# A hybrid decoder layer on one core: memory's first quarter in two pieces, the first weight slice scaled on VectorE

## The chip, the core and the metric

The kernel runs on one core of a Trainium2 chip. The core has TensorE (PE, matrix products; its weight loads are shown as PEld), VectorE (DVE), ScalarE (ACT), GpSimd (POOL) and SyncE (SP), which here only issues transfers. Engines run side by side and wait for each other by semaphores; the queue of each engine is in order. SBUF is the working memory, PSUM the memory of eight banks into which TensorE writes. The metric is the device time of one execution in microseconds.

## The reference

One layer with three groups of heads side by side, a residual and a final norm:

```python
h = rmsnorm(x, ln_g)                        # x: 1024 x 2048
proj = h @ w_in                             # columns split among the groups
out_a = gmlp_spatial_gating(...) * silu(g_z)            # 4 groups x 128
out_b = rmsnorm(gated_delta_rule(...)) * silu(d_z)      # 8 heads x 128, a recurrence over chunks of 64
m = rmsnorm(mem, mem_norm_g)                # mem: 256 x 2048
mk, mv = split(m @ w_mem_kv)                # keys and values of the memory, 4 heads x 128 each
out_c = softmax(c_q @ mk.T / sqrt(128)) @ mv * silu(c_z)
y = rmsnorm(x + concat(out_a, out_b, out_c) @ w_out, final_g)
```

All data is float32. The change touches the product `m @ w_mem_kv`.

## The kernel before

Matrix products are made from pairs of rounded numbers: every operand `t` is split into a high part `hi` (rounded to the type float32r by a cast) and a low part `lo = t - hi`, and `triple` (line 465) issues three products, hi by hi, hi by lo and lo by hi, into the same PSUM bank. Splitting is done by `split_to` (line 442): a cast on ScalarE, then a subtraction on VectorE.

The program isn't issued as it is written. Every instruction goes into a list (`Plan.add`, line 138) with its estimated cost, its rank and what it depends on; `Plan.issue` (line 228) plays the list through, engine by engine, always taking the ready instruction of the lowest rank, and then issues all of them in that order (line 297, the line that the profile shows for nearly everything). The order on each engine is fixed from then on. Since it comes from one sweep over all estimated times, an edit at the start can change the order far behind it.

The work around the change is the start of the kernel, the memory stage:

- `load_mem(q)` (line 495) loads quarter `q` of the memory's 2048 columns: two tiles of 128 rows by 512 columns, called `kT` (rows 0 to 127) and `qT` (rows 128 to 255) in the profile, 256 KB each, both issued by SyncE. Lines 516 to 525 set the order: quarter 0, the gain `mem_norm_g` on ScalarE's queue (8 KB), weight slices 0 and 1, quarter 1, weight slices 2 and 3, quarters 2 and 3.
- Seven small products of a tile of ones (`warm`, line 540) keep TensorE occupied until the gain is there; the gain is transposed into `gcol`, one column for each slice of 128 input columns.
- `spread_mem(q)` (line 546) transposes a quarter on TensorE, four 128x128 blocks into one PSUM bank for each of the two row tiles. Two banks, `dn_111` and `dn_112`, take turns for this (`spare`, line 530). Each bank is split into the high part (a tile of the ring `gt`) and the low part (a tile of the ring `inv`).
- The loop at line 595 runs over the 16 weight slices `k`, 128 rows by 1024 columns each (512 KB). `load_kv` loads a slice into one of four buffers (two `wraw`, two `ut`), slice 0 as two halves; ScalarE scales it by the gain into `whi`, VectorE computes the low part `wlo` from the raw slice, the gain and `whi`; TensorE does 12 products of 256 columns for the keys (banks `acc`) and 6 of 512 columns for the values (banks `dn`). Two buffers hold `whi` and `wlo` in turn, so slice k + 2 waits for the products of slice k.
- In between stand the squares of the memory's rows for its norm (ScalarE, `jk`), and `prep` (line 557): x's row tiles (`vs`, `kd`, then `kT`, `qT` again) are loaded, squared, scaled, transposed through the same two banks and, for the first half of x's rows here, copied to `tn`, split and written out (`put0`). `spare`'s two banks thus are shared by memory, x and a few small products.

Behind the memory stage follow the wide projections (`acc<-ahi,whi` and its like), cut into blocks, with the delta rule's inverses (`dn<-inv`), its scan (`dn<-tblk,gt`, `dn<-states,kT`, `dn<-steps,...`) and the spatial gate (`dn<-wsT,el`) strewn between their products, then attention and the output projection.

Of the kernel before, what the change touches and what calls it, by code (L numbers as in the profile page):

```python
# [11 lines left out]
AF = mybir.ActivationFunctionType  # L12
ALU = mybir.AluOpType
# [4 lines left out]
P = 128  # L18
# [4 lines left out]
HT = 512  # L23
# [37 lines left out]
class Plan:  # L61
# [27 lines left out]
    @contextmanager  # L89
    def rank(self, cls):  # L90
        old, self.cls = self.cls, cls
        yield
        self.cls = old

    @contextmanager
    def behind(self, op):
        old, self.gate = self.gate, op
        yield
        self.gate = old
# [201 lines left out]
def kernel(  # L301
# [21 lines left out]
    x, mem, w_in, out = x[0], mem[0], w_in[0], out[0]  # L323
# [7 lines left out]
    V, S, G, PE, Q = R.dve, R.act, R.pool, R.pe, R.sp  # L331
    rank, behind = R.rank, R.behind

    def C(shape, name, dt=F32):
        return sb.tile(list(shape), dt, name=name, tag=name)[:]
# [44 lines left out]
    def tok(ap):  # L380

        return ap.rearrange("p (t c) -> p t c", c=P)
# [38 lines left out]
    def tpb():  # L421
        turn["tp"] += 1
        return acc[2 + turn["tp"] % 2]
# [5 lines left out]
    ident, ones, utri = (C([P, P], n) for n in ("ident", "ones", "utri"))  # L429
# [12 lines left out]
    def split_to(hi, lo, src, eng):  # L442
        S.copy(hi, src)
        eng.tensor_tensor(out=lo, in0=src, in1=hi, op=ALU.subtract)
# [20 lines left out]
    def triple(a, l, r, start, stop, cls=9):  # L465

        mm(a, l[0], r[0], start, False, cls)
        mm(a, l[0], r[1], False, False, cls)
        return mm(a, l[1], r[0], False, stop, cls)
# [4 lines left out]
    def row_scale(xq):  # L474

        s = small()
        for c in range(4):
            S.activation(jk, xq[c], AF.Square, accum_out=s[:, c : c + 1])
        V.tensor_reduce(s[:, 4:5], s[:, 0:4], axis=AX.X, op=ALU.add)
        V.tensor_scalar(s[:, 4:5], s[:, 4:5], 1.0 / D, EPS, op0=ALU.mult, op1=ALU.add)  # L480
        rsqrt_to(s[:, 5:6], s[:, 4:5])
        return s[:, 5:6]


    def row_tiles(tag):
        if tag in ("inv", "gt", "ut"):
            return [b[:, i * HT : (i + 1) * HT] for b in (ring[tag](), ring[tag]()) for i in range(2)]
        return [ring[tag]() for _ in range(4)]
# [3 lines left out]
    mem_rows = [row_tiles("kT"), row_tiles("qT")]  # L492
    x_rows = {}

    def load_mem(q):
        for mt in range(2):
            Q.dma_start(mem_rows[mt][q], mem[mt * P : (mt + 1) * P, q * HT : (q + 1) * HT])

    def kv_parts(k):
        n = XW if k == 0 else 2 * XW  # L500
        return [slice(i, i + n) for i in range(0, 2 * XW, n)]

    def load_kv(k):
        for sl in kv_parts(k):
            Q.dma_start(kvraw[k % 4][:, sl], w_mem_kv[k * P : (k + 1) * P, sl])

    def load_x(tt, tag, after=(None,) * 4):
        x_rows[tt] = row_tiles(tag)
        for c in range(4):
            with behind(after[c] or R.gate):  # L510
                Q.dma_start(x_rows[tt][c], x[tt * P : (tt + 1) * P, c * HT : (c + 1) * HT])
# [2 lines left out]
    rows = y1.rearrange("p c m -> p (c m)")[:, 0:P]  # L514
    mrow = rows[0:16]
    with rank(2):
        load_mem(0)
        S.dma_start(mrow, mem_norm_g[0].rearrange("(c p) -> c p", p=P))
        for k in range(4):
            load_kv(k)  # L520
            if k == 1:
                load_mem(1)
    with rank(3):
        load_mem(2)
        load_mem(3)
# [4 lines left out]
    def spare():  # L530
        turn["dn"] = 1 - turn["dn"]
        return flip[turn["dn"]]
# [10 lines left out]
    gcol = C([P, 16], "gcol")  # L543
    with rank(1):
        V.tensor_copy(gcol, pt[:, 0:16])
    def spread_mem(q):
        h, l = (ring[t](F32R).rearrange("p (k n) -> p k n", k=4) for t in ("gt", "inv"))
        for mt in range(2):
            tp = spare()
            for k in range(4):  # L550
                PE.transpose(tp[:, k * P : (k + 1) * P], mem_rows[mt][q][:, k * P : (k + 1) * P], ident)
            sl = slice(mt * P, (mt + 1) * P)
            with rank(2):
                split_to(h[:, :, sl], l[:, :, sl], tok(tp), V)
        return h, l

    def prep(tt, put, bank):

        xq = x_rows[tt]
        r = row_scale(xq)  # L560
        for q in range(NQ):
            V.scalar_tensor_tensor(xq[q], xq[q], r, gb[q], op0=ALU.mult, op1=ALU.mult)
            tp = bank()
            for k in range(4):
                PE.transpose(tp[:, k * P : (k + 1) * P], xq[q][:, k * P : (k + 1) * P], ident)
            put(q, tok(tp))
# [8 lines left out]
    def put0(tt):  # L575
        def put(q, tp):
            if tt >= H0:
                with rank(1):
                    split_to(ahq[q][:, tt], alq[q][:, tt], tp, V)
                return  # L580
            t = tok(ring["tn"]())
            with rank(1):
                S.copy(t, tp)
            with rank(2):
                split_to(ahq[q][:, tt], alq[q][:, tt], t, V)
            with rank(5):
                Q.dma_start(h0_d[4 * q : 4 * q + 4, :, tt * P : (tt + 1) * P].rearrange("k p n -> p k n"), t)

        return put


    rm = []
    kvmark = []
    mhl = [spread_mem(0)]
    for k in range(KT):
        mh, ml = mhl[k // 4]
        if k >= 4:
            with rank(3):
                load_kv(k)
        hi, lo = kvhi[k % 2], kvlo[k % 2]  # L600
        with rank(2):
            for sl in kv_parts(k):
                raw = kvraw[k % 4][:, sl]
                S.activation(hi[:, sl], raw, AF.Copy, scale=gcol[:, k : k + 1])
                V.scalar_tensor_tensor(lo[:, sl], raw, gcol[:, k : k + 1], hi[:, sl], op0=ALU.mult, op1=ALU.subtract)
        kk = k % 4
        for h in range(NX):
            sl = slice(h * P, (h + 1) * P)
            triple(ka[h][:, :NMEM], (hi[:, sl], lo[:, sl]), (mh[:, kk], ml[:, kk]), k == 0, k == KT - 1)
        for mt in range(2):  # L610
            sl = slice(mt * P, (mt + 1) * P)
            triple(va[mt], (mh[:, kk, sl], ml[:, kk, sl]), (hi[:, XW:], lo[:, XW:]), k == 0, k == KT - 1)
        kvmark.append(R.ops[-1])
        if k == 3:
            with rank(2), behind(kvmark[-1]):
                for c in range(4):
                    Q.dma_start(gb[c], ln_g[0, c * HT : (c + 1) * HT].partition_broadcast(P))
        if k in (1, 4, 8):
            with behind(kvmark[-1]):
                mhl.append(spread_mem(len(mhl)))  # L620
        if k == 1:
            load_x(0, "vs", kvmark[1:2] * 4)
        if k == 3:
            for mt in range(2):
                rm.append(C([P, 1], f"rm{mt}"))
                V.tensor_copy(rm[mt], row_scale(mem_rows[mt]))
        if k == 4:
            load_x(1, "kd", kvmark[4:5] * 4)
        if k == 5:
            prep(0, put0(0), spare)  # L630
        if k == 7:

            dg, rmb = (ring["E"]()[:, 0:NMEM] for _ in range(2))
            for mt in range(2):
                V.tensor_scalar(dg[:, mt * P : (mt + 1) * P], ident, rm[mt], None, op0=ALU.mult)
            pt = spare()
            PE.matmul(pt[:, 0:NMEM], ones, dg, start=True, stop=True)
            S.copy(rmb, pt[:, 0:NMEM])
        if k == 9:
            prep(1, put0(1), spare)  # L640
            load_x(2, "kT", (kvmark[6], kvmark[7], kvmark[7], kvmark[8]))
        if k == 13:
            load_x(3, "qT", (kvmark[10], kvmark[11], kvmark[11], kvmark[12]))
            with rank(2):
                prep(2, put0(2), spare)
# [584 lines left out]
    a = tpb()  # L1230
# [23 lines left out]
    a = tpb()  # L1254
# [564 lines left out]
```

## Time and profile before

| | us |
|---|---|
| three runs | 1626.97, 1629.00, 1629.74 |
| median | 1629.0 |
| profiled execution, its own time | 1630.94 |
| span of the profile (first to last instruction) | 1629.2 |
| TensorE busy | 1611.6 |
| VectorE busy | 1262.2 |
| ScalarE busy | 1027.0 |
| GpSimd busy | 300.3 |

A row of the order of time reads: start, duration, engine, line, operation, output <- inputs, shapes, count, and in brackets the idle time of the engine before it and what ended that. An engine's name with a q (SPq) is an instruction of its queue, the issue of a transfer; the transfer itself lands later. In the waits each row names who waited for whom, with the total, the number of times and the longest. A view by stretches gives for each engine the busy time within a stretch and the number of instructions, then the TensorE clock that was granted, the mean busy share of the DMA engines and the transferred GB/s. Matrix instructions overlap, so their durations add up to more than the time between their starts.

### The profile page before, as it was taken

Reading aid. Unit: us, or ns where it says so; the run is one execution under the profiler, and the core shown is the slowest. Engines: PE = TensorE matmul, PEld = TensorE weight load, DVE = VectorE, ACT = ScalarE, POOL = GpSimd, SP = SyncE. Lnnn points to the kernel's source line nnn. Section 1 sums busy time; section 2 is a strip of 40 time slices with the busy share of each in tenths; the row PEclk is TensorE's granted clock in tenths of the full one; section 3 lists DMA queues with packets and bytes.
Section 4 is the critical chain, followed back from the end, with each engine's and each line's share of the span. In section 5 each row is a group of like instructions: output and inputs, shape, how many; then the busy total and the mean of one; then the engine's idle time right before and its main releaser. Section 6 shows DMA issues by size and latency. Waiting matters only on the chain.

```text
span 1629.2 us, 26133 instructions
## 1 busy us (share of the span) xinstructions
PE 1611.6 (99%) x8576; PEld 1354.8 (83%) x8576; DVE 1262.2 (77%) x2100; ACT 1027.0 (63%) x2217; POOL 300.3 (18%) x482
## 2 busy tenths in 40 slices
PE   8999999999999999999999999999999999999997
PEld 8988888888888888888888788888888888888886
DVE  5966787879756567899988897768768888789775
ACT  6767675765475457888685346766666775344355
POOL 0101220351452010225235005330100000000001
PEclk9999999999999999999999999999999999999999
DMA  9867898988977785689878977878968869688646
GB/s 309 241 179 225 280 301 251 278 282 309 359 257 242 261 283 190 204 286 368 281 243 253 320 228 241 266 265 296 319 201 274 282 218 364 207 273 293 218 146 239
DMA packets 277227, 428.94 MB, mean 263 GB/s; under 512 B 31017, under 2 KB 102242, under 8 KB 277090
## 3 DMA queue, kind: packets, MB, share of 16 engines
q1 hardware_dynamic: 254338, 366.81, 68.7%
q0 software_dynamic: 22144, 59.40, 10.9%
q8 instruction: 67, 1.10, 0.3%
q10 hardware_dynamic: 608, 1.06, 0.2%
q14 instruction: 70, 0.57, 0.1%
HBM read 339.57 MB, written 87.06 MB: 262 GB/s over the span
## 4 chain that ended last, share of the span: by engine, by line
PE 89%; DMA 6%; DVE 2%; issue 1%; ACT 1%; SPq 1%; POOLq 0%; POOL 0%; DVEq 0%; ACTq 0%
PE acc L297 69%; PE dn L297 20%; DMA wraw<-in_w_in_dram 1%; SPq L297 1%; DMA vs<-od 1%; DMA kT<-in_mem_dram 1%; DVE alo L297 0%; DMA wraw<-hTd 0%; DVE y L297 0%; DMA ai<-in_w_in_dram 0%; DMA kd<-in_x_dram 0%; DMA y<-in_w_in_dram 0%; DMA wraw<-in_w_out_dram 0%; DMA pd<-y 0%; DMA wraw<-in_w_mem_kv_dram 0%
## 5 line engine op out<-in xcount | busy, mean ns | idle before, releaser
L297 PE MATMUL acc<-ahi,whi 128*128 128x512 f32 (+1 forms) x1512 | 535.5, 392 | 0.0
L297 PE MATMUL acc<-ahi,wlo 128*128 128x512 f32 (+1 forms) x1144 | 446.9, 391 | 0.0
L297 PEld LDWEIGHTS acc<-ahi,whi 128*128 128x128 f32 x1512 | 283.2, 188 | 53.9
L297 PE MATMUL acc<-alo,whi 128*128 128x512 f32 (+1 forms) x776 | 302.1, 389 | 0.2 <-DVE alo L297 0.2
L297 PEld LDWEIGHTS acc<-ahi,wlo 128*128 128x128 f32 x1144 | 215.2, 188 | 41.0 <-DVE wlo L297 0.4
L297 ACT CAST whi<-wraw 128x512 fp32r<-128x512 f32 (+1 forms) x167 | 134.2, 804 | 129.1 <-PE acc L297 86.7
L297 DVE TENSOR_TENSOR wlo<-wraw,whi 128x512 fp32r<-128x512 f32 (+1 forms) x167 | 154.0, 922 | 60.7 <-ACT whi L297 56.9
L297 ACT CAST ahi<-raws 128x1024 fp32r<-128x1024 f32 x130 | 136.3, 1049 | 61.2 <-PE acc L297 26.9
L297 PEld LDWEIGHTS acc<-alo,whi 128*128 128x128 f32 x776 | 146.0, 188 | 27.6 <-DVE alo L297 0.6
L297 PE MATMUL acc<-ahi,zl 128*128 128x512 f32 x376 | 148.2, 394 | 0.0
L297 PE MATMUL acc<-alo,zh 128*128 128x512 f32 x376 | 148.2, 394 | 0.0
L297 PE MATMUL acc<-ahi,zh 128*128 128x512 f32 x376 | 148.1, 394 | 0.0
L297 POOL TENSOR_TENSOR small<-small,mhalf 128x1 f32<-128x1 f32 x26 | 18.0, 696 | 590.9 <-DVE small L297 578.0
L297 DVE TENSOR_TENSOR alo<-raws,ahi 128x1024 fp32r<-128x1024 f32 x65 | 79.3, 1220 | 19.7 <-ACT ahi L297 19.5
L297 DVE TENSOR_TENSOR ahi<-raws,ahi 128x1024 fp32r<-128x1024 f32 x65 | 79.2, 1219 | 18.2 <-ACT ahi L297 17.9
L297 DVE TENSOR_TENSOR alo<-y,ahi 128x1024 fp32r<-128x1024 f32 x65 | 79.2, 1219 | 15.7 <-ACT ahi L297 15.4
L297 ACT CAST ahi<-y 128x1024 fp32r<-128x1024 f32 x65 | 68.1, 1048 | 35.1 <-PE dn L297 19.2
L297 PEld LDWEIGHTS acc<-ahi,zl 128*128 128x128 f32 x376 | 70.7, 188 | 13.8
L297 PEld LDWEIGHTS acc<-ahi,zh 128*128 128x128 f32 x376 | 70.7, 188 | 13.8
L297 PEld LDWEIGHTS acc<-alo,zh 128*128 128x128 f32 x376 | 70.7, 188 | 13.8
L297 PE MATMUL acc<-whi,ahi 128*128 128x512 f32 x232 | 79.7, 391 | 0.0
L297 PE MATMUL dn<-whi,ahi 128*128 128x512 f32 x216 | 74.1, 389 | 0.0
(422 smaller groups left out, 3414.3 us busy)
## 6 DMA issues: line engine op xcount, KB each, us to landing
wraw<-in_w_in_dram SPq DMA_DIRECT2D x268, 256.0 KB, 4.0
raws<-sd SPq DMA_DIRECT2D x150, 256.0 KB, 4.1
y<-in_w_in_dram SPq DMA_DIRECT2D x92, 256.0 KB, 4.7
y<-sd SPq DMA_DIRECT2D x75, 256.0 KB, 3.6
wraw<-in_w_out_dram SPq DMA_DIRECT2D x64, 256.0 KB, 4.7
raws<-h0d SPq DMA_DIRECT2D x54, 256.0 KB, 5.1
y<-in_w_out_dram SPq DMA_DIRECT2D x33, 256.0 KB, 4.8
sd<-zg SPq DMA_DIRECT2D x32, 256.0 KB, 4.0
```

The costliest lines, as they stand in the source:

```text
L297: o.fn(*o.args, **o.kw)
```

## The change

Quarter 0 of the memory is loaded in two pieces, columns 0 to 127 first, its second row tile's piece by ScalarE's queue, and the other 384 columns behind weight slice 0. Quarter 1 is loaded behind slice 2 instead of behind slice 1. The first piece is transposed and split by itself: one bank for both row tiles, 256 columns; the rest follows as two banks of 384 columns. The high part of weight slice 0 is made by VectorE (`tensor_scalar`) instead of ScalarE; slices 1 to 15 stay as they are.

```diff
-    def load_mem(q):
+    def load_mem(q, a=0, b=HT, queues=(Q, Q)):
         for mt in range(2):
-            Q.dma_start(mem_rows[mt][q], mem[mt * P : (mt + 1) * P, q * HT : (q + 1) * HT])
+            queues[mt].dma_start(mem_rows[mt][q][:, a:b], mem[mt * P : (mt + 1) * P, q * HT + a : q * HT + b])
...
     with rank(2):
-        load_mem(0)
         S.dma_start(mrow, mem_norm_g[0].rearrange("(c p) -> c p", p=P))
+        load_mem(0, 0, P, (Q, S))
         for k in range(4):
             load_kv(k)
-            if k == 1:
+            if k == 0:
+                load_mem(0, P)
+            if k == 2:
                 load_mem(1)
...
         h, l = (ring[t](F32R).rearrange("p (k n) -> p k n", k=4) for t in ("gt", "inv"))
+        if q == 0:
+            tp = spare()
+            for mt in range(2):
+                PE.transpose(tp[:, mt * P : (mt + 1) * P], mem_rows[mt][q][:, 0:P], ident)
+            with rank(2):
+                split_to(h[:, 0], l[:, 0], tp[:, 0 : 2 * P], V)
+        ks = slice(1 if q == 0 else 0, 4)
         for mt in range(2):
             tp = spare()
-            for k in range(4):
+            for k in range(ks.start, 4):
                 PE.transpose(tp[:, k * P : (k + 1) * P], mem_rows[mt][q][:, k * P : (k + 1) * P], ident)
             sl = slice(mt * P, (mt + 1) * P)
             with rank(2):
-                split_to(h[:, :, sl], l[:, :, sl], tok(tp), V)
+                split_to(h[:, ks, sl], l[:, ks, sl], tok(tp)[:, ks], V)
...
-                S.activation(hi[:, sl], raw, AF.Copy, scale=gcol[:, k : k + 1])
+                if k == 0:
+                    V.tensor_scalar(hi[:, sl], raw, gcol[:, k : k + 1], None, op0=ALU.mult)
+                else:
+                    S.activation(hi[:, sl], raw, AF.Copy, scale=gcol[:, k : k + 1])
```

In the order that the planner makes of it, TensorE's instructions are the same 7848 (a transposition or product each) in another order up to about 1000 us of the run before, and in the same order behind that.

## The prediction

> **What bounds the kernel now.** I read the page's busy shares first, then the chain that ended last, then TensorE by stretches of time, and its waits last.
>
> ```profile
> PE 1611.6 (99%) x8576; PEld 1354.8 (83%) x8576; DVE 1262.2 (77%) x2100; ACT 1027.0 (63%) x2217; POOL 300.3 (18%) x482
> ...
> PE 89%; DMA 6%; DVE 2%; issue 1%; ACT 1%; SPq 1%; POOLq 0%; POOL 0%; DVEq 0%; ACTq 0%
> ```
>
> TensorE is busy for all but 17.6 us, and 89% of the chain is its own work. The change leaves that work alone: both programs hold the same 7848 matrix instructions. Time can move only in TensorE's waits and in its clock, so the next view is where those lie (columns: stretch; length, busy time and count of each engine; granted clock; DMA share; GB/s).
>
> ```profile
> 3.60:7.00 3.40, 3.00 (x13) 2.20 (x12) 0.67 (x2) 1.83 (x5) 0.00 (x0) 1.00 0.99 324
> 7.00:10.45 3.45, 2.83 (x11) 2.64 (x12) 2.59 (x5) 2.37 (x5) 0.00 (x0) 1.00 1.00 343
> 34.40:37.80 3.40, 1.47 (x11) 1.07 (x10) 1.95 (x2) 3.40 (x10) 0.00 (x0) 1.00 0.97 389
> 37.80:41.20 3.40, 3.40 (x16) 3.22 (x15) 2.25 (x4) 3.40 (x7) 0.00 (x0) 0.50 0.98 236
> 62.00:1000.00 938.00, 934.09 (x4981) 783.23 (x4979) 742.03 (x1320) 607.96 (x1398) 247.86 (x389) 1.00 0.82 266
> 1000.00:1629.00 629.00, 619.63 (x3243) 519.57 (x3242) 479.78 (x720) 372.82 (x731) 46.11 (x79) 1.00 0.76 256
> ```
>
> Three things are seen. The memory stage at the start, with the DMA engines full (0.97 to 1.00). A hole at 34.4 to 37.8 us (1.93 us idle), after which the clock stands at 0.50 for 3.4 us. And from 62 to 1000 us only 938.00 - 934.09 = 3.9 us idle, spread over a few waits:
>
> ```profile
> PE dn L297 <- ACT tn L297: 1.9, 1, 1.9
> PE dn L297 <- DMA el<-vd: 1.7, 1, 1.7
> PE acc L297 <- ACT gt L297: 0.9, 1, 0.9
> PE dn L297 <- ACT vs L297: 0.9, 1, 0.9
> PE dn L297 <- POOL gt L297: 0.4, 1, 0.4
> ```
>
> **The change, part 1: the first slice (k = 0).** Rows before, from the order of time:
>
> ```profile
> 3.12 0.43 SPq L297 DMA_DIRECT2D kT<-in_mem_dram  x1
> 4.74 1.12 PE L297 MATMUL dn<-ident,kT 128*128 128x128 f32 x4
> 5.64 1.06 PE L297 MATMUL dn<-ident,qT 128*128 128x128 f32 x4
> 5.89 0.58 ACT L297 CAST gt<-dn 128x512 fp32r<-128x512 f32 x1 [0.45 <-PE dn L297]
> 6.37 0.72 ACT L297 ACTIVATE whi<-wraw,gcol 128x512 fp32r<-128x512 f32 x1
> 6.51 0.69 DVE L297 TENSOR_TENSOR inv<-dn,gt 128x512 fp32r<-128x512 f32 x1 [1.67 <-ACT gt L297]
> 7.62 1.22 PE L297 MATMUL acc<-gt,whi 128*128 128x256 f32 x4 [0.92 <-ACT gt L297]
> 8.40 0.74 DVE L297 SCALAR_TENSOR_TENSOR wlo<-wraw,gcol,whi 128x512 fp32r<-128x512 f32 x1
> 9.71 0.41 PE L297 MATMUL acc<-gt,wlo 128*128 128x256 f32 x1
> 11.81 0.28 PE L297 MATMUL acc<-gt,whi 128*128 128x256 f32 x1
> ```
>
> Before, ScalarE does cast, scale, cast, scale in a row, 0.6 to 0.7 us each, and the first matmul starts at 7.62. After, the first piece needs two transposes, one cast of 256 columns and one scaled half slice. A cast of 256 columns costs 0.38 us (the 256-column copy below) instead of 0.58. The scaling moves to VectorE, where before had no such instruction at the start; the nearest row is a scaled 128x512 tile near the end at 0.48 us, the other bound is the three-operand form at 0.74. I take 0.48, the same operation and shape.
>
> ```profile
> y<-in_mem_norm_g_dram ACTq DMA_DIRECT2D x1, 8.0 KB, 3.4
> ...
> 44.22 0.38 ACT L297 COPY E<-dn 128x256 f32<-128x256 f32 x1
> ...
> 1614.85 0.48 DVE L297 TENSOR_SCALAR kT<-kT,small 128x512 f32<-128x512 f32 x1
> ```
>
> The Trainium skill, VectorE: DVE Perf Modes (section "The perf-mode tier table"), says that a one-source fp32 operation between SBUF tiles streams two elements a cycle and a two-tensor one only one; the row 0.48 against 0.74 agrees.
>
> The smaller load helps little: 8 KB took 3.4 us to land, and 256 KB were there for the transposes at 4.74, so the 64 KB piece gains 0 to 0.5 us. The half for mt = 1 moves to ScalarE's queue, behind the gain's load and ahead of its table load, with nothing else waiting there yet. SyncE issues one transfer more, 0.43 us, hidden: it issues ahead of the landings here, with the DMA engines full. With transposes at 4.6 and 0.25 us each (8 in 2.0 us), gt stands at about 5.6, and the first matmul starts at 5.8 to 6.4, 1.2 to 1.8 us sooner.
>
> Little of that is kept. Until about 10.4 us TensorE runs slow (0.41 us for 256 columns at 9.71, 0.28 later; start to start 0.21 against 0.12; the clock column holds 1.00 there, so I go by the durations). All of slice 0 now waits for pieces: three matmuls, three transposes of the rest, one matmul, three more transposes. From 6.0: 12 x 0.21 + 6 x 0.25 = 4.0 us of slow work to 10.0, 0.2 of waiting, then six 512-column matmuls (one at the slow 0.43, five at 0.23) to about 11.7. Before, slice 0 ended at 11.81. Gain 0.1, bounds 0 to 0.8 (half of the first start's gain). VectorE gets more: two scalings (0.96) and three subtractions for two; its last low half ends at about 8.9 against 9.14, so TensorE doesn't see it. ScalarE loses two scalings and gains one cast.
>
> **Part 2: memory's second quarter one slice later.** In the new order slice 2's weights land ahead of that quarter. Slices 1 and 2 follow slice 0 without a hole in either kernel, so this hides; without that cover it would cost the landing of one 256 KB transfer, 0.7 us. Slice 3 had this wait:
>
> ```profile
> 18.86 0.38 PE L297 MATMUL acc<-gt,wlo 128*128 128x256 f32 x1 [0.15 <-DVE wlo L297]
> ...
> 33.83 0.63 ACT L297 ACTIVATE jk<-kd 128x512 bf16<-128x512 f32 x1 [4.34 <-DMA kd<-in_x_dram]
> 34.46 1.13 ACT L297 ACTIVATE whi<-wraw,gcol 128x1024 fp32r<-128x1024 f32 x1
> 36.11 0.56 ACT L297 COPY tn<-dn 128x512 f32<-128x512 f32 x1
> 36.73 0.66 PE L297 MATMUL dn<-ident,vs 128*128 128x128 f32 x4 [1.93 <-ACT tn L297]
> ```
>
> Its weights are now scaled one 0.75 us square sooner on ScalarE, so the wait (0.15 in that row, 0.3 with the late start around it) goes. TensorE comes to the wall at 34.8 us about 0.4 us sooner.
>
> **Part 3: the wall.** ScalarE sat 4.34 us for x's second row tile (kd); the copy that frees a PSUM bank stood behind it. That transfer was held by its queue, which issues it behind weights that wait for a buffer, so 0 to 0.9 us of the start's gain reaches it. In the new order two kd tiles go ahead of a 512 KB weight load, but all four squares now stand ahead of the copy, where one, a scaling and a second stood. The fourth tile's landing decides: I put the copy at 35.3 to 36.3 (it was at 36.11). Four matmuls of slice 8 now stand ahead of the waiting transposes, 0.5 us already done. Gain of the whole start, set here: 0.5 + 0.4 = 0.9, bounds -0.5 (fourth tile late) and 1.9 (hole gone). It isn't added to the gains in front of it: the wall swallows those.
>
> The hole left is 1.0 to 2.0 us. Before, 1.93 idle of 3.40 was followed by a stretch at clock 0.50, which costs half of 3.4, 1.7 us. I keep that drop, at no change; bounds -1.7 (gone) and +1.7 (a second one).
>
> **Part 4: the rest of the order.** The planner's order is rewritten from there to about 1000 us; behind it TensorE's order is the same row for row, so the waits and the tail there stay. Which of the waits above survive is read from the two orders:
>
> ```profile
> 439.09 1.10 PE L297 MATMUL dn<-tblk,gt 128*128 128x64 f32 x8 [0.42 <-POOL gt L297]
> 456.64 1.05 PE L297 MATMUL dn<-states,kT 128*128 128x128 f32 x4 [0.88 <-ACT vs L297]
> ...
> 916.60 0.60 PE L297 MATMUL dn<-ident,ut 128*128 128x128 f32 x4
> ...
> 925.71 1.13 PE L297 MATMUL dn<-wsT,el 128*128 128x128 f32 x8 [1.68 <-DMA el<-vd]
> ```
>
> At 925.71 TensorE reads a tile that was written out after the transposes at 916.60 and read back. Between the two stood 6.8 us of matmuls; now 11.1 us (30 and 49 instructions at 0.23). The 1.68 us go. At 439.09 the scan waits for GpSimd's chain; it now stands some 15 us of matmuls later, so 0.4 goes. At 456.64 the pair stands as close as before: stays. Against that, some 5000 instructions stand in a new order whose waits no row of before shows. Bounds: none, and twice the 3.9 of before; I take 1.5, the size of one of its larger waits, nearer the low end because the scan's own spacing is the same in both orders.
>
> **Sum**: -0.9 - 1.7 - 0.4 + 1.5 = -1.5 us. The profiled execution took 1630.94 us around its span of 1629.2, 1.9 over the median of the runs shown (1629.0), which lie 2.8 us apart; I set the difference against the median: 1627.5 us. Differences under 0.2% (3.3 us) are about what a measurement of this kernel can't tell from none.
>
> **Rivals.**
> Nothing arrives: the wall stands where the kd transfer lands and new waits equal those lost: 1629.0. For it: DMA share 0.97 at the wall. Against: the 925.71 spacing.
>
> No clock drop: the shorter hole leaves the clock at 1.00; -1.5 - 1.7 gives 1625.8. For it: 1.0 us idle of 3.4 is under the 1.93 that preceded the drop. Against: it can be 2.0. By the Trainium skill, TensorE: Matmul & The Clock Gate (section "Why this matters for your kernels"), gaps under about 3 us leave the clock alone; here 1.93 us of gap was followed by 0.50, so by that rule the time would be this rival's, and the trace doesn't bear it out.
>
> A clean new order: all 3.9 us of waits between 62 and 1000 gone and none new, drop kept: -0.9 - 3.9 gives 1624.2. Against: six places with four different causes.
>
> The scan late: it begins 15 us of matmuls later and the late inverses 20 to 40 us later, yet from 1000 us the order is fixed, so its slack is spent, and its steps wait for the engine that prepares them as at 456.64, 0.88 us each. With eight such waits: -0.9 - 1.7 - 0.4 + 7.0 = +4.0, 1633.0; from a little over seven on it is slower by over 0.2%. For it: there are 56 steps. Against: before shows one such wait.
>
> **How the numbers follow.** Small gain as summed 0.40 (its own range 1625 to 1630); nothing arrives 0.09; no clock drop 0.14; clean order 0.13; scan late 0.24. Faster by over 0.2%, under 1625.7: clean order, half of no drop, 0.06 of the first, 0.26. Slower, over 1632.3: nearly all of scan late and 0.03 of the first, 0.26. Within: 0.48. The range 1622.8 to 1634.5 goes past each rival's time and leaves out some 0.06 below and 0.12 above.
>
> **What would show it.** The first acc matmul at 5.8 to 6.4 us, slice 1 still starting at 11 to 11.8; no wait on wlo near 18 us; the transposes of x's third quarter at 35.4 to 36.8 and a stretch at clock 0.50 behind; no wait of over 0.5 us for el<-vd near 925; idle time from 62 to 1000 us of 2 to 5 us. Wrong if that idle time is over 8 us, if the wall moves later than 37.5, or if the clock drops twice.

## The result, and the profile after

The changed kernel takes 1640.97 us (median of 7 runs, 1632.04 to 1642.56), the kernel before, measured beside it, 1628.57 us (7 runs, 1624.98 to 1629.74). The ratio is 1.007, with a 95% interval of 1.005 to 1.009: slower by about 11 us. The forecast was 1627.5 us, with a range up to 1634.5. The profiled execution of the changed kernel took 1641.15 us, its span is 1639.4 us; against the profile before, with its span of 1629.2 us, 10.2 us are to be found.

The page of the changed kernel, busy shares and the chain that ended last:

```profile
PE 1616.1 (99%) x8576; PEld 1356.8 (83%) x8576; DVE 1262.5 (77%) x2103; ACT 1024.0 (62%) x2214; POOL 293.4 (18%) x482
...
PE 84%; DMA 6%; issue 4%; DVE 3%; ACT 2%; POOL 1%; SPq 0%; POOLq 0%; ACTq 0%; DVEq 0%
```

TensorE is busy for 4.5 us more with the same instructions, which is what a slow clock does, and idle for 23.3 us of the span instead of 17.6. The view by stretches of the changed kernel (columns as before: stretch; length, busy time and count of PE, PEld, DVE, ACT, POOL; granted clock; DMA share; GB/s) says where:

```profile
3.60:7.00 3.40, 2.50 (x14) 1.80 (x13) 2.29 (x6) 0.82 (x2) 0.00 (x0) 1.00 0.82 228
7.00:10.45 3.45, 1.54 (x9) 1.40 (x8) 1.07 (x2) 1.09 (x5) 0.00 (x0) 0.65 0.99 378
10.45:13.90 3.45, 3.45 (x12) 2.97 (x12) 1.84 (x2) 1.79 (x4) 0.00 (x0) 0.50 1.05 408
34.40:37.80 3.40, 3.40 (x27) 3.15 (x26) 2.83 (x6) 3.37 (x9) 0.00 (x0) 1.00 1.02 398
37.80:41.20 3.40, 3.40 (x25) 3.04 (x24) 3.30 (x5) 3.40 (x6) 1.10 (x1) 1.00 0.99 283
62.00:1000.00 938.00, 928.27 (x4873) 776.62 (x4871) 735.48 (x1312) 598.96 (x1383) 236.25 (x379) 0.99 0.81 262
1000.00:1639.40 639.40, 629.65 (x3340) 527.76 (x3338) 484.84 (x728) 378.14 (x742) 51.98 (x89) 0.99 0.77 257
```

The start is rougher than before (1.91 us idle in the second row, then half the clock), the hole at 34.4 to 37.8 us is gone and the clock behind it is full. And from 62 to 1000 us TensorE is idle for 938.00 - 928.27 = 9.7 us, where it was 3.9. TensorE's waits of the changed kernel in that part (60 to 1000 us), the largest:

```profile
PE dn L297 <- DMA el<-vd: 4.1, 1, 4.1
PE dn L297 <- DMA ut<-udrearly: 2.6, 1, 2.6
PE acc L297 <- DVE wlo L297: 0.7, 1, 0.7
PE acc L297 <- DVE tn L297: 0.6, 1, 0.6
PE dn L297 <- DVE ai L297: 0.6, 1, 0.6
```

Two waits make 6.7 of the 9.7 us, and behind each the clock falls. The stretches around them, changed kernel:

```profile
451.79:455.20 3.41, 1.69 (x51) 1.47 (x52) 2.25 (x4) 0.90 (x4) 1.40 (x4) 1.00 1.07 293
455.20:458.61 3.41, 3.41 (x10) 2.64 (x9) 2.22 (x4) 2.68 (x5) 2.70 (x6) 0.50 0.85 256
929.65:933.07 3.42, 1.02 (x5) 0.52 (x3) 0.96 (x6) 1.99 (x2) 1.19 (x2) 1.00 1.00 356
933.07:936.48 3.41, 1.74 (x9) 1.77 (x9) 0.00 (x0) 0.00 (x0) 0.00 (x0) 0.50 1.01 353
936.48:939.89 3.41, 3.41 (x10) 2.73 (x10) 2.55 (x4) 0.00 (x0) 0.00 (x0) 0.50 0.77 293
```

At clock 0.50 products of 512 columns start 0.43 us apart (936.5 to 939.9 us), elsewhere 0.23, so half of the work time there is lost: (3.41 + 1.74 + 3.41) / 2 = 4.3 us. The waits that are more than before, 9.7 - 3.9 = 5.8 us, and the clock, 4.3 us, make 10.1 us between 62 and 1000 us.

To see when the loss arises I laid the two profiles over each other by work: the time at which TensorE has done the same amount of matrix work. Measured so, the changed kernel is some 2 us late at 14 to 34 us, 1.7 us ahead at 42 and 1.5 at 62 us, within 1 us of level from 80 to 420 us, about 3 us late at 600, 4.7 at 880, 9.6 at 960, 11.1 at 1040 and 10.3 us late at the end. (TensorE's order differs on the way, so the figures between 420 and 600 us depend on how small products are weighed.) So the start, all that the change edits, ends ahead or level; the whole loss comes 400 us and more behind it.

### The profile page after: what moved, and what is told of

Its sections match the earlier page's. It is cut to its first block, busy times and chain, and to the rows that moved or that the text cites. A ratio compares the mean times of both kernels' runs of the same rounds, so it can differ in the third digit from the quotient of the medians.

```text
span 1639.4 us, 26130 instructions
## 1 busy us (share of the span) xinstructions
PE 1616.1 (99%) x8576; PEld 1356.8 (83%) x8576; DVE 1262.5 (77%) x2103; ACT 1024.0 (62%) x2214; POOL 293.4 (18%) x482
## 4 chain that ended last, share of the span: by engine, by line
PE 84%; DMA 6%; issue 4%; DVE 3%; ACT 2%; POOL 1%; SPq 0%; POOLq 0%; ACTq 0%; DVEq 0%
PE acc L297 63%; PE dn L297 20%; DMA y<-in_w_in_dram 1%; DMA wraw<-hTd 1%; DVE wlo L297 1%; ACT whi L297 1%; DVE tn L297 1%; DMA tdrearly<-inv 0%; ACT ahi L297 0%; DMA qT<-in_x_dram 0%; DMA kT<-in_x_dram 0%; DMA qT<-in_mem_dram 0%; DMA ut<-udrearly 0%; DVE alo L297 0%; DMA kd<-in_w_in_dram 0%
## 5 line engine op out<-in xcount | busy, mean ns | idle before, releaser
L297 DVE TENSOR_TENSOR alo<-y,ahi 128x1024 fp32r<-128x1024 f32 x65 | 79.7, 1227 | 17.9 <-ACT ahi L297 17.6
```

Source lines behind the costliest of these rows:

```text
L297: o.fn(*o.args, **o.kw)
```

## The experiments

Theory A: the loss is in the order of issue that the planner drew behind the start, and the edited work is harmless. Theory B: the loss comes from the edited start. To tell them apart, one edit replaces the planner's last step, in kernels whose work is not touched, by a given order in which all dependences still hold:

```diff
-        self.ops.sort(key=lambda o: (o.at, o.idx))
+        order = given_order()
+        ops = {o.idx: o for o in self.ops}
+        self.ops = [ops[i] for i in order]
```

**The changed start, the old order behind 60 us** (the edit above, in the changed program).

> The changed program, all three parts of the change in it, with the changed kernel's issue order up to the planner's 60 us and the issue order of the kernel before behind that. Theory A (the loss lies in the re-planned order behind the memory stage: waits for el<-vd and ut<-udrearly and the two stretches at clock 0.50 behind them; the start itself ends ahead): 1626 to 1628 us, 1.7 us or so under the kernel before, idle time from 62 to 1000 us about 4 us, no clock of 0.50 between 60 and 1630 us. Theory B (the loss comes from the start: the late second piece of memory's rows, the slow clock of slice 0, the work added to VectorE): 1638 to 1641 us, whatever order follows.

Measured: 1626.53 us against 1627.13 for the kernel before, ratio 0.9996 (0.9987 to 1.0005). All of the change is in it, and none of the loss. Its view by stretches has 2.8 us idle from 62 to 1000 us, and no half clock:

```profile
62.00:1000.00 938.00, 935.17 (x4985) 784.31 (x4984) 741.06 (x1319) 608.08 (x1399) 248.70 (x390) 1.00 0.82 267
```

**The old start, the new order behind 60 us** (the same edit, in the program before).

> The program of the kernel before, with its own issue order up to the planner's 60 us and the changed kernel's issue order behind that; none of the three parts of the change is in it. Theory A (order): 1638 to 1643 us, with waits of 3 us or more for el<-vd near 930 us and for ut<-udrearly near 453 us and the clock at 0.50 behind each. Theory B (start): 1628 to 1630 us.

Measured: 1638.49 us, ratio 1.0067 (1.0055 to 1.0079). None of the change is in it, and nearly all of the loss. Its waits on TensorE from 60 to 1000 us:

```profile
PE dn L502 <- DMA el<-vd: 3.7, 1, 3.7
PE dn L502 <- DMA ut<-udrearly: 1.8, 1, 1.8
PE dn L502 <- ACT vs L502: 1.2, 2, 0.9
```

The second is smaller than I had put it. Together the two runs leave theory B no room: the order behind the start makes the loss.

**One part alone.** Memory's second quarter one slice later, alone, leaves TensorE's planned order as it was; each of the two other parts alone brings nearly the changed kernel's. Both were run.

```diff
 (only_scale: the kernel before with)
+                if k == 0:
+                    V.tensor_scalar(hi[:, sl], raw, gcol[:, k : k + 1], None, op0=ALU.mult)
+                else:
+                    S.activation(hi[:, sl], raw, AF.Copy, scale=gcol[:, k : k + 1])
 (only_split: the kernel before with)
+        load_mem(0, 0, P, (Q, S))
...
+            if k == 0:
+                load_mem(0, P)
```

> The kernel before with one part of the change alone, the first slice's high part scaled on VectorE; memory is loaded and transposed as before. Its planned order from 60 to 1000 us is the changed kernel's but for 273 of 7848 matrix instructions, 3 us later. Theory A (order): 1636 to 1642 us, with the waits for ut<-udrearly and el<-vd. Theory B (the loss comes from the two-piece load): 1627 to 1630 us.

> The kernel before with one part of the change alone: memory's first quarter loaded and transposed in two pieces; the scaling stays on ScalarE, the second quarter's place stays. Its planned order is the changed kernel's but for 23 of 7848 places. Theory A (order): 1636 to 1642 us with the waits for ut<-udrearly and el<-vd. Theory B (the loss comes from the scaling on VectorE): 1627 to 1630 us.

Measured: 1638.64 us (ratio 1.0068, 1.0052 to 1.0083) and 1638.89 us (1.0068, 1.0056 to 1.0081). The waits for ut<-udrearly and el<-vd are in both, in all 0.8 and 4.0 us in the one, 0.8 and 4.4 us in the other. Two edits that share no instruction cost the same: they tip the planner into nearly the same order.

**Another order by another number.** If any new order costs, so should one that comes from the planner's own settings.

```diff
-    SLACK = 600.0
+    SLACK = 650.0
```

> The kernel before with one number of its planner changed (the distance it keeps between a result and the matmul that reads it, 600 to 650), no work changed; 3314 of the 7848 matrix instructions then stand at another place. Theory A (any re-planning draws a new set of waits, of either sign and of several us): the time moves by more than 2 us, to 1631 or more or to 1626 or less, and the idle time from 62 to 1000 us differs from 3.9 us by more than 1.5 us. Theory B (the order as such costs nothing much): within 1 us of 1628.6 us.

Measured: 1626.62 us, ratio 0.9995 (0.9987 to 1.0004). Theory A falls in the form that I gave it here: 3314 instructions moved, and the time didn't. A new order need not cost anything; the changed kernel's does. Then the changed kernel with another order should lose nothing:

> The changed kernel, all three parts, with the planner's distance at 650 instead of 600. No work differs; behind 60 us its planned order of matrix instructions is that of the kernel before with 650, which took 1626.6 us, but for 250 of 7848 places, and its scan's first write udrearly is planned at 411.7 us (the changed kernel: 426.4, the kernel before: 412.1). Theory A (the order behind the start makes the loss, the start is harmless): 1624.5 to 1628 us, no wait over 1.3 us from 60 to 1000 us and no clock of 0.50 there. Theory B (the changed start costs, or any order planned behind it does): 1634 us or more.

> The changed kernel with the planner's distance at 700: a third order, 4947 places off the changed kernel's, planned to end at 1616.7 us by the planner's own clock (the changed kernel: 1614.5, the kernel before: 1615.4). Theory A: its time follows the waits that it draws, which the planned end does not tell; the scan's first write is planned at 407.4 us, as far ahead as in the good orders, so 1625 to 1631 us. Rival (the planner's own end tells): 2.2 us over the changed kernel, 1641 to 1643 us.

Measured: 1628.28 us with 650, ratio 1.0001 (0.9993 to 1.0010), and 1633.34 us with 700, ratio 1.0029 (1.0019 to 1.0039). With 650 the whole change costs nothing (the time is 0.3 us over theory A's 1628, and one wait of 2.0 us, for `steps`, is over what I allowed; the clock stays full). With 700 it loses 5 us, by other waits than the changed kernel's, 2.2 us for `kT` with half a clock behind it and 1.6 us for `states`; neither theory had named 1633. The planner's own ends (1615.0 us for 650, 1616.7 for 700, 1614.5 for the changed kernel, 1615.4 for the kernel before) rank the slowest of these four first, so they don't tell the time.

**What is late at 934.74 us?** In the changed kernel, SyncE's queue between the writes of `vd` and the reads that TensorE waits for:

```profile
918.39 2.04 SPq L297 DMA_DIRECT2D vd<-states  x4
920.68 0.33 SPq L297 DMA_DIRECT2D kd<-in_w_in_dram  x1
...
926.44 1.47 SPq L297 DMA_DIRECT2D ai<-in_w_in_dram  x2
928.62 0.33 SPq L297 DMA_DIRECT2D pd<-y  x1
929.46 0.33 SPq L297 DMA_DIRECT2D el<-vd  x1
930.13 0.32 SPq L297 DMA_DIRECT2D tn<-vd  x1
```

and TensorE's row:

```profile
934.74 2.05 PE L297 MATMUL dn<-wsT,el 128*128 128x128 f32 x8 [4.07 <-DMA el<-vd]
```

The read `el<-vd` goes out 9.0 us behind the last write (920.43 to 929.46); before, it was 5.2 us (914.89 to 920.12), with ten others between:

```profile
912.51 2.38 SPq L297 DMA_DIRECT2D vd<-states  x4
...
920.12 0.70 SPq L297 DMA_DIRECT2D el<-vd  x1
```

In the changed kernel twelve other transfers stand between, some of them waiting for buffers. Four kernels move reads forward in the given order of the changed program:

```diff
 (after_el_early)      vd<-states x4, el<-vd, 12 others, tn<-vd
 (after_reads_early)   vd<-states x4, el<-vd, tn<-vd, 12 others
 (after_ut_first)      GpSimd: tblk x3, ut x4, tblk x3, ut ...  (was: tblk x6, ut x7 ...)
 (after_both_early)    both of the last two
```

> The changed kernel with one instruction moved: the read el<-vd that the matmuls at 934.74 us waited for is issued right behind the writes that it reads back, ahead of the 12 other transfers that stood between on SyncE's queue. Theory A (the read stood too late in SyncE's queue): it goes out at about 922.5 instead of 929.5 us, the 4.07 us wait goes, the clock stays at 1.00 behind it (3.4 us), the 0.9 us wait at 943 or so may stay: 1633.5 to 1636 us. Rival (the write's landing, not the queue, sets it, or the next late thing takes its place): 1639 to 1641 us.

Measured: 1639.72 us, ratio 1.0076 (1.0061 to 1.0091): the rival. The read went out at 918.88, its products ran at 926.37 without a wait, and 7 us later the next read of the same pair was as late as the first had been:

```profile
928.21 0.33 SPq L502 DMA_DIRECT2D tn<-vd  x1
933.38 1.54 PE L502 MATMUL dn<-wsT,tn 128*128 128x128 f32 x8 [4.10 <-DMA tn<-vd]
```

> The changed kernel with two entries of SyncE's queue moved: both reads, el<-vd and tn<-vd, right behind the writes that they read back. (With el<-vd alone moved the wait passed to tn<-vd, issued at 928.21 us.) Theory A (the pair of reads stood behind ten loads): no wait over 0.6 us at 925 to 940 us, clock 1.00 behind it, 5 to 7.5 us less than the changed kernel: 1632.5 to 1635.5 us. Rival (what follows in the same chain is as late, as it was with one read moved): 1638 to 1641 us.

Measured: 1634.88 us, ratio 1.0048 (1.0035 to 1.0061). Some 5 us less than the changed kernel, as theory A had it, but not for the whole reason: a wait of 2.72 us stayed, now for VectorE. Its rows in that kernel:

```profile
925.03 0.69 DVE L502 TENSOR_TENSOR kT<-kT,wraw 128x512 f32<-128x512 f32 x1 [5.88 <-DMA wraw<-in_w_in_dram]
...
930.30 0.74 DVE L502 SCALAR_TENSOR_TENSOR el<-dn,col,bt 128x512 f32<-128x512 f32 x1
...
931.09 2.08 PE L502 MATMUL dn<-wsT,tn 128*128 128x128 f32 x8 [2.72 <-DVE el L502]
```

VectorE stood 5.88 us for a load that SyncE had issued at 920 to 921 us, then worked off twelve operations before it came to the evacuation of `el` that TensorE waited for. So what is late on SyncE's queue reaches TensorE by two ways, the read itself and VectorE's queue.

> The changed kernel with four entries of GpSimd's queue exchanged: four reads ut<-udrearly, the tile that the matmuls at 453.51 us waited for, stand three places sooner, ahead of three reads tblk<-tdrearly that are needed later. Theory A (GpSimd's queue, which lets eight reads out and then pauses 1.0 and 2.5 us, holds the eighth read that TensorE needs): that read goes out at about 442 instead of 447.3 us, the 2.6 us wait and the 3.4 us at clock 0.50 behind it go: 4.3 us less than the changed kernel's 1639 to 1641 us, so 1634.5 to 1637 us. Rival (something else of the same chain is as late): the wait moves by a few instructions and the time stays.

Measured: 1639.07 us, ratio 1.0068 (1.0054 to 1.0082): the rival. The fourth read goes out by 443.4 us, the wait for `ut` is gone, and twelve products later stands a new one, for the tile that GpSimd passes on:

```profile
457.16 1.10 PE L502 MATMUL dn<-tblk,gt 128*128 128x64 f32 x8 [2.20 <-POOL gt L502]
```

> The changed kernel with both edits, the four reads ut<-udrearly and the two reads of vd sooner in their queues; TensorE's own order is the changed kernel's, unchanged. Theory A (the loss is these two waits and the clock behind them): 1628 to 1631 us, within 0.2% of the kernel before. Rival (the loss is spread over the new order): 1635 us or more.

Measured: 1633.81 us, ratio 1.0042 (1.0029 to 1.0055), between the two forecasts. Both named reads are early; in the profile, waits of 1.7 us for GpSimd and 3.0 us for VectorE's `el` remain (its execution took 1638.28 us, the longest of the five, so the others may have waited less). The place of these reads in their queues thus explains about half of the loss. The other half I read as TensorE's own order asking for the results of these two chains too soon; no run moved its products apart.

**Where in the order does the wait near 930 us arise?** In the changed kernel the delta rule's scan begins 14 us later by the planner's clock (in the profiles its first write is issued at 432.36 us, before at 415.10). Theory P: the order around 930 us makes the wait. Theory Q: it is carried there from the late scan. Four kernels change from one order to the other at a later place, by the same edit of the order.

> The program of the kernel before, with its own order up to the planner's 700 us and the changed kernel's order behind that. Theory P (order around the wait): the wait of 3 us or more near 925 to 935 us is there, 1633 to 1638 us. Theory Q (carried from the late scan): no such wait, 1627 to 1630 us.

> As the last, with the change of order at the planner's 860 us. Theory P, cause in the last 140 us of the new order: the wait near 930 us stays, 1633 to 1638 us. Theory P, cause between 700 and 860 us, or theory Q: 1627 to 1630 us.

Measured: 1635.24 us (ratio 1.0044, 1.0033 to 1.0056) and 1636.21 us (1.0047, 1.0029 to 1.0065). With the old order for the first 860 us the wait is there all the same; the waits of old860_new from 60 to 1000 us begin

```profile
PE dn L503 <- DMA el<-vd: 3.5, 1, 3.5
PE dn L503 <- ACT vs L503: 0.8, 1, 0.8
```

That is theory P, with the cause of this wait in the last 140 us of the new order. These two kernels lose 7.2 and 7.6 us of the 11, so most of the loss arises there. The rest, some 4 us, is about what the wait near 450 us and the half clock behind it cost in the changed kernel's profile (2.57 + 1.7 us).

> The changed program, with the changed kernel's order up to the planner's 700 us and the order of the kernel before behind that. Theory P (the wait near 930 us is made by the order around it): only the loss at 450 us stays, 1629 to 1633 us, no wait over 2 us near 920 to 930 us. Theory Q (it is carried there: the scan begins 14 us later in the new order and never makes it up): the wait near 925 us stays at 3 us or more, 1636 to 1641 us.

> The changed program, with the changed kernel's order up to the planner's 860 us and that of the kernel before behind. Theory P, cause in the last 140 us: no wait over 2 us near 930 us, 1629 to 1633 us. Theory P with the cause between 700 and 860 us, or theory Q: the wait stays, 1636 to 1641 us.

Measured: 1645.29 us (ratio 1.0104, 1.0084 to 1.0123) and 1636.53 us (1.0060, 1.0042 to 1.0078). The first result misses both theories; the second lies where theory Q had it, but not by the wait that it names. Joining the orders this way round makes a wait of its own at the joint: in new700_old TensorE is idle for over 11 us between 706 and 722 us, in new860_old for 4.4 us up to 870 us. Neither has any wait in which TensorE stood between 880 and 1000 us, though the scan is late in both. That speaks against theory Q, but weakly, since a stall at the joint also lets the other queues catch up. What refutes it is the pair before: there the wait stands without the late scan.

**Can the start be made better?** The second piece of qT was late in the changed start. In this kernel, with the planner at 650, the second pieces go out ahead of the first weights:

```diff
             if k == 0:
+                load_mem(0, P)
             load_kv(k)
-            if k == 0:
-                load_mem(0, P)
```

> As after_slack650, with the second pieces of memory's first quarter issued ahead of the first slice's weights instead of behind them. Theory: the wait for the second piece of qT (0.8 to 2.3 us at 7 to 9 us in the runs of the changed start, with the clock at 0.50 behind it in most) goes, the first weights land up to 1 us later; 0 to 3 us less than after_slack650: 1623 to 1627 us. Rival (the memory stage is bound by its transfers, so what the start gains is lost by 36 us): the same as after_slack650 within 1 us.

Measured: 1626.60 us, ratio 0.9995 (0.9986 to 1.0003). The wait for the transfer is gone, but TensorE then waits 1.52 us for VectorE (`inv`) at the same place. The time is 1.7 us under after_slack650, with intervals that overlap, and equal to the kernel before. No version here beats the kernel before by what can be measured.

## Why the prediction was wrong

**Part 4, the rest of the order, is the step that failed**, twice. From 62 us on it said -1.7 for the wait at 925.71, -0.4 for the one at 439.09 and +1.5 for new ones, -0.6 together; the overlay of the profiles, 1.5 us ahead at 62 and 10.3 late at the end, gives about +11.8.

*The wait for el<-vd.* I took the 4.3 us of matrix work added between the transposes at 916.60 and the products at 925.71 for slack. But `el` is read from the tile `vd` of the first half of the rows, which was written before those transposes (the last write had been issued by 914.89); the transposes belong to the other half. The distance that counts is the one from the last write, through SyncE's queue, to the read's landing, and I didn't follow that queue, though the read stood in it behind ten others. There the distance grew, from 5.2 to 9.0 us, while the time that TensorE gave it, from the last write's issue until it stood idle, grew only from 9.1 us (914.89 to 924.03) to 10.2 (920.43 to 930.67). The wait was to go; it grew from 1.68 to 4.07 us, and took the clock with it.

*The new waits.* The 1.5 us had bounds of nothing and 7.8 us. TensorE's idle time grew by 5.8 us; counted as the forecast counted, with 2.1 us of old waits taken off, that is 7.9 us of new ones, at the upper bound, where I had taken a value near the low end. What the bounds left out was the clock: I priced it at one place, the hole at 34.8 us, and at no other, and between 62 and 1000 us 4.3 us were lost. The range's upper end, 1634.5 us, went 1.5 us past the scan's rival (1633.0), which carried no clock from there on either.

*The wait at 439.09.* It went, as forecast; in its place the scan's read `ut<-udrearly` was late by 2.57 us. The order gave TensorE 18.3 us from the scan's first write to that product instead of 19.9 (415.10 to 435.04 before; 432.36 to 450.70 in the changed kernel).

**The rival "scan late"** had the right sign, and the wait near 450 us is for a read of the late scan. Its mechanism was wrong: the waits for the engine that prepares the scan's steps (`vs`) are 0.9 us in all, not seven or eight of 0.88 us. The late work was transfers and what VectorE and GpSimd do with them, and the larger wait, near 930 us, is there without the late scan (old860_new). **"Nothing arrives"** was right in one thing only: the fourth `kd` load landed when it did before, at 35.39 us against 35.41.

**Part 1.** The changed start's own rows:

```profile
4.87 0.98 DVE L297 TENSOR_SCALAR whi<-wraw,gcol 128x512 fp32r<-128x512 f32 x2
5.51 0.59 PE L297 MATMUL acc<-gt,whi 128*128 128x256 f32 x3 [0.49 <-ACT gt L297]
6.10 1.41 DVE L297 SCALAR_TENSOR_TENSOR wlo<-wraw,gcol,whi 128x512 fp32r<-128x512 f32 x2
6.50 0.55 PE L297 MATMUL dn<-ident,kT 128*128 128x128 f32 x3 [0.40 <-DMA kT<-in_mem_dram]
9.08 0.87 PE L297 MATMUL dn<-ident,qT 128*128 128x128 f32 x3 [1.91 <-DMA qT<-in_mem_dram]
```

The first product at 5.51 us (forecast 5.8 to 6.4), two scalings at 0.49 us (0.48) and the last low half at 7.5 us (8.9) came as well as forecast or better. The term "0.2 of waiting" failed: behind the first product it was 0.40 + 1.91 = 2.3 us. I had costed the landing of the first pieces and of nothing behind them. The chain shows what I had missed, the second piece of qT:

```profile
2.65 6.29 DMA qT<-in_mem_dram
```

It landed at 8.94 us, and the clock went to half from 8.05 to 14.88 us, so that all six 512-column products ran at the slow 0.43 us of which I had reckoned one. Slice 0 ended at 14.02 us, not at 11.7. This piece landed at another time in every run: the wait for it was from nothing to 2.5 us in the other profiles of the same start.

**Part 2** held: no wait on `wlo` is left near 18 us. **Part 3** held in its place and failed in its effect. The copy that frees the bank stands at 36.20 us, within the forecast 35.3 to 36.3, but not for the reason given: the fourth `kd` load was there at 35.39 us, and ScalarE, at work with hardly a gap from 33.05 us on, came to its square only at 35.57. TensorE came to the wall some 2 us late, so its 1.93 us of idle time became nothing, and the drop that I kept at 1.7 us went with it. With -1.7 us at 42 us, the head is inside its bounds (-0.5 to +1.9 of gain), but by luck and not by the forecast's way; waits at 62 to 73 us (`whi` 0.17, `wlo` 0.70) took 0.9 us of it back, and at 80 us the kernels were level.

The signs that I gave for "wrong" were the right ones: idle time over 8 us from 62 to 1000 us, and a clock that drops twice.

## What to carry to other kernels

Where an order is planned in one sweep, an edit is priced by what the planner does with it: compare the whole new order with the old one, and follow each read-back from its write through the issuing queue to its landing, not the matrix work in front of its reader. Let the same work run under one or two other orders before an edit is called good or bad; here the same change cost 11 us under one order, 5 under another and nothing under two more. Price each new wait of 2 us or more with a possible clock drop beside it, 1.7 us for each stretch of 3.4 us at half clock.

## What the runs showed of the hardware

The clock. Behind the start, holes in TensorE's work of 1.8 to 4.4 us were followed by stretches at clock 0.50, but not each time. In after_el_early and only_scale, two holes that were larger than the 1.93 us before, 2.82 and 3.66 us, left the clock alone. All the stretches at 0.50 but the one at the end of each run are 3.41 us long or a multiple of it (6.83, once 13.65). Cut into pieces of 3.41 us in step with its stretches, the trace of after_el_early shows the hole shared by two pieces (the third row is the piece behind):

```profile
445.83:449.24 3.41, 1.76 (x9) 1.07 (x7) 2.95 (x5) 2.11 (x4) 3.32 (x6) 1.00 1.04 356
449.24:452.65 3.41, 2.15 (x53) 1.85 (x54) 1.78 (x3) 1.35 (x5) 1.44 (x3) 1.00 1.07 286
452.65:456.07 3.42, 3.42 (x20) 2.66 (x19) 2.72 (x4) 2.87 (x6) 2.99 (x7) 1.00 0.73 231
```

and so does that of only_scale:

```profile
923.03:926.44 3.41, 1.58 (x7) 0.96 (x6) 1.52 (x7) 1.99 (x2) 1.18 (x2) 1.00 1.06 400
926.44:929.86 3.42, 1.59 (x11) 1.54 (x12) 0.42 (x1) 0.00 (x0) 0.00 (x0) 1.00 1.05 401
929.86:933.27 3.41, 3.41 (x21) 2.94 (x20) 3.22 (x7) 0.00 (x0) 0.00 (x0) 1.00 0.95 344
```

The 1.93 us before lay whole in one piece. Cut like this, behind the first 15 us and ahead of the last 10, the 18 traces of this case have 14 pieces at full clock in which TensorE was idle for 1.87 us or more, and 0.50 followed each of them. It followed no piece with 1.71 us or less; in between it followed 1.73 and 1.76 us, but not 1.83, 1.84 and 1.85. So what counts here is less a hole's length than how much of it falls into one piece. The pieces begin at another time in every trace (borders at 4.64 us in the changed kernel's, at 10.48 in that before), so whether a hole of 1.9 to 3.7 us costs its clock is partly luck. What decides between 1.7 and 1.87 us stayed open.

The Trainium skill, TensorE: Matmul & The Clock Gate (section "Why this matters for your kernels"), lets gaps under about 3 us pass. The runs agree with it in neither direction: 1.93 us before and 2.57 us in the changed kernel were followed by 0.50, and 3.66 us in only_scale was not.

GpSimd's queue. It issued eight reads, then one after a pause of 1.0 us, then paused 2.5 us more before the next (changed kernel):

```profile
438.65 3.37 POOL L297 DMA_DIRECT2D tblk<-tdrearly  x6 [5.75 <-DMA tdrearly<-inv]
442.00 1.17 POOL L297 DMA_DIRECT2D ut<-udrearly  x2
444.18 0.58 POOL L297 DMA_DIRECT2D ut<-udrearly  x1 [1.02 <-DMA tblk<-tdrearly]
447.29 2.26 POOL L297 DMA_DIRECT2D ut<-udrearly  x4 [2.53 <-issue]
```

With the order of the reads exchanged, the pauses, 0.6 and 2.6 us, stood behind the eighth and the ninth read again, whichever tile they belonged to. The profile puts the end of the first pause down to the landing of one of the reads before; what sets the second it doesn't show.

The spread. The changed kernel's runs lie 10.5 us apart, those of the kernel before 4.8 us. The mean granted clock of every run is on record too. Over the seven runs of the changed kernel it comes to 8.2 us lost on average (one minus the clock, times the run), over the 23 runs of the kernel before that were taken beside the first experiments to 3.3 us: 4.9 us more, close to the 4.3 us of the one profile. But the clock alone doesn't explain the spread: the changed kernel's run of 1640.97 us had a mean clock of 0.998, its fastest, of 1632.04 us, one of 0.996.
